# One over the rms of x by a transposed write and a broadcast read, V's tiles at another offset, the last row pair in banks of its own, and a reciprocal with a fixed place

## The chip, the cores and the metric

The kernel runs on one core of a Trainium2 chip. The time is the device time of one execution in microseconds (us), the median of three runs. A core has five engines with instruction streams of their own: TensorE (PE, matrix products; its weight loads are listed as PEld), VectorE (DVE), ScalarE (ACT), GpSimd (POOL) and SyncE (SP), which mainly starts DMA transfers. An engine runs its stream in order; streams wait for each other through semaphores. PE writes its results into eight PSUM banks of 128 partitions by 512 float32, which DVE and ACT read.

## The reference

One layer of a hybrid encoder on x of 512 tokens by 2048 features, batch 1:

```python
h = rms_norm(x, norm_w)                       # 1/sqrt(mean(x*x)) per token, times norm_w
proj = h @ w_in                               # 2048 -> 4608: q | k | v | gate | lru input | lru gate
attn_out = attention_group(q, k, v, ...)      # 8 heads, 2 kv heads, head size 128, qk-norm, axial rope
lru_out = lru_group(xr, ...)                  # conv of 4 taps, two gated scans, forward and backward
mixed = concat(rms_norm(attn_out) * silu(g_attn), rms_norm(lru_out) * silu(g_lru))
out = x + mixed @ w_out                       # 2048 -> 2048
```

All arrays are float32, and the result is wanted in nearly that precision.

## The kernel before, in words

Every matrix operand is split into a high part (rounded to the float32r format, which PE takes in one pass) and a low part (the rest), and every product is three matmuls: high by high, high by low, low by high (`mm3`, lines 153 to 155, and `product`, line 1035). A weight chunk is 256 rows by 512 columns: SP loads it (`wraw`, line 206) into a ring of three slots (`wr`), ACT writes the high part (`wh`, line 218) and DVE the low part (`wl`, line 219). A chunk is 24 matmuls of a projection.

The projections run one after another on PE, whose instruction order is the written one: the lru input in two halves of 512 columns (`a1` and `a2`), k and v, q in two halves, then the lru gates and the attention gates, which are woven with the attention; last the output product, which goes by seven products of half size (Strassen's scheme) with sums of weights built by DMA. x itself comes in eight chunks of 256 features. They are turned to features by tokens, by PE (line 253) or by 32 by 32 block transposes and a round trip through DRAM (lines 281, 289, 296), and split in two (line 339), while `a1` is already being computed from them.

x is not scaled by 1/rms before the projection. The factor is applied to the result when it leaves PSUM: per partition, where tokens lie on partitions (`rstd`, 128 by 4), and by a full tile `rbc` (128 by 512, the same row of 512 token factors on each partition), where tokens lie along the row (`evac_bc`, line 471). `rows` makes `rbc` from `rstd`: DVE splits `rstd` (lines 357, 358), multiplies an identity by each column (line 360, two 128 by 512 tiles), PE sums them over the partitions with a matrix of ones (line 367, two matmuls), and DVE copies the bank to `rbc` (line 368). Its first part is issued at step (4, 3) of `a1` (chunk 4, column block 3), the matmuls at step (7, 0). Seven small loads of vectors (`vec_load`, line 180, into `vec_st`) are issued at step (4, 2), turned by PE at step (7, 1) (line 189).

`a2` takes the four PSUM banks that `a1` leaves, so that its first matmul needs the first `evac_bc` of `a1`.

Attention works by heads. Per head and block of 128 queries: scores (`mm<-kt,q`), maximum, exponent, division, a block transpose, and a round trip through DRAM (`u`, `pd`, `pt`) that gives the weights as keys by queries, split in `ph` and `pl`. `values` multiplies them with V: twelve matmuls per head whose stationary operand is V's high or low tile (`mm<-ph,v`). V's tiles come from `aside`, which takes a tile of 528 floats and uses the 512 that begin 8 floats (32 bytes) in.

`spread` gives the factors of the two group norms: two matmuls with ones (line 831), a square root by ACT (832), and four reciprocals of 128 columns by DVE (835). The second use is in the last gate projection, from `later()`. The order of ACT and DVE is made there by a planner, by priorities; `issue_after` and `behind` put one instruction behind another of the same engine, without a wait.

At the end of the output product, three products Q3, P2 and Q4 of the right-hand columns finish one after another, each with its last two of eight steps and a closing addition by DVE from PSUM (line 1066) and a store (line 1058). Each has two banks, one per 128 rows of the pair. For Q4, the last, the second bank's addition is cut in two column halves, the first stored through ACT's queue and the second through SP's. Here ACT, DVE, SP and POOL also run in the written order.

Of the kernel before, what the change touches and what calls it, by code (L numbers as in the profile page):

```python
# [11 lines left out]
F32 = mybir.dt.float32  # L12
F32R = mybir.dt.float32r
# [4 lines left out]
P = 128  # L18
SEQ = 512
DM = 2048  # L20
KT = DM // P
NT = SEQ // P
HD = 128
NH = 8
NKV = 2
# [11 lines left out]
AHEAD = 600  # L37
# [11 lines left out]
H = 256  # L49
# [14 lines left out]
def hybrid_kernel(  # L64
# [53 lines left out]
    def nm(s):  # L118
        cnt[0] += 1
        return f"{s}_{cnt[0]}"  # L120
# [4 lines left out]
    def k2(dt=F32, shape=(P, SEQ)):  # L125
        return pools["lru"].tile(list(shape), dt, tag="k2", bufs=LRU_K2, name=nm("k2"))
# [13 lines left out]
    def pj():  # L140
        return ps.tile([P, SEQ], F32, tag="pj", name=nm("pj"))

    def mm():
        return ps.tile([P, SEQ], F32, tag="mm", name=nm("mm"))

    def const(shape, name, dt=F32):
        return cp.tile(list(shape), dt, tag=name, name=name)
# [22 lines left out]
    def vec_load():  # L170
        for lo, src in (
            (R_CW, conv_w.rearrange("t o (n p) -> (t o n) p", p=P)),
            (R_CB, conv_b.rearrange("(n p) -> n p", p=P)),
            (R_BA, lru_ba.rearrange("d (n p) -> (d n) p", p=P)),
            (R_BX, lru_bx.rearrange("d (n p) -> (d n) p", p=P)),
            (R_LAM, lru_lambda.rearrange("d (n p) -> (d n) p", p=P)),
            (R_AN, attn_norm_w.rearrange("(n p) -> n p", p=P)),
            (R_LN, lru_norm_w.rearrange("(n p) -> n p", p=P)),
        ):
            nc.sync.dma_start(vec_st[lo : lo + src.shape[0], :], src)  # L180
# [62 lines left out]
    def behind(those):  # L243
        stack = ExitStack()
        for ins in those:
            stack.enter_context(tc.issue_after(ins))
        return stack
# [101 lines left out]
    rstd = const([P, NT], "rstd")  # L349
    rbc = const([P, SEQ], "rbc")  # L350

    def rows(dst, col, dg):

        shape = [P, NT, P]
        part = [const([P, NT], nm("part")) for _ in range(2)]
        parts = [dg() for _ in part]
        nc.vector.tensor_copy(part[0].bitcast(F32R), col)
        nc.vector.tensor_sub(part[1], col, part[0])
        for c, d in zip(part, parts):
            nc.vector.tensor_mul(  # L360
                d, ident[:, None, :].broadcast_to(shape), c[:, :, None].broadcast_to(shape)
            )
        yield
        pb = mm()
        for k, d in enumerate(parts):
            d = d.rearrange("p t q -> p (t q)")
            nc.tensor.matmul(pb, ones_r, d, start=k == 0, stop=k == 1)
        nc.vector.tensor_copy(dst, pb)
        yield

    def xstats():
        s = const([P, NT], "xsum")
        nc.vector.reduce_sum(s, ssq, axis=AX.X)
        rsqrt_mean(rstd, s, DM, NT)
        yield from rows(rbc, rstd, lambda: k2(F32R, (P, NT, P)))

    def proj_feat(c0, acc, first=None, given={}, take=None):

# [273 lines left out]
    def kv(es):  # L654
        turned_k = sent(norm_rope(es, NKV, rk), NKV)
        yield 20
        opened("wx", "right")
        for t in range(NT):
            vv = es[t][:, NKV * HD :]
            vt = aside(  # L660
                lambda *a: pools["qkv"].tile(*a, tag="v", bufs=NT, name=nm("v")), 2 * NKV * HD // H
            )
            vh[t], vl[t] = vt[:, 0, :], vt[:, 1, :]
            nc.scalar.copy(vh[t], vv)
            nc.vector.tensor_sub(vl[t], vv, f(vh[t]))
        yield from lru_squares()
        yield 2
        drain(turned_k)
        yield 6
        pair = landed(asides.pop(0))  # L670
        for h in range(NKV):
            yield (12, 4)[h]
            kt = pools["qkv"].tile([P, 2, SEQ], F32R, tag="kt", bufs=NKV, name=nm("kt"))
            kth[h], ktl[h] = kt[:, 0, :], kt[:, 1, :]
            those = split_head(pair, h, kth[h], ktl[h])
        parts = halved(
            sums["l"],
            lambda: pools["rope"].tile([P, SEQ], F32R, tag="kv", bufs=NT, name=nm("kv")),
            those,
        )  # L680
        yield 4
        spread(gbc, parts, NB * P)
# [141 lines left out]
            nc.vector.tensor_sub(lo, src, f(hi))  # L824
        return hi, lo

    def spread(dst, parts, n):

        pb = mm()
        for k, part in enumerate(parts):  # L830
            nc.tensor.matmul(pb, ones_r, part, start=k == 0, stop=k == 1)  # L831
        nc.scalar.activation(dst, pb, AF.Sqrt, scale=1.0 / n, bias=eps[:, :1])
        for t in range(NT):
            ts_ = slice(t * P, (t + 1) * P)
            nc.vector.reciprocal(dst[:, ts_], dst[:, ts_])  # L835

    gbc = const([P, SEQ], "gbc")

# [12 lines left out]
    def seven(pair, hi, lo):  # L851
# [7 lines left out]
        for to, part in ((slice(0, 3), src[:, 1:4]), (slice(3, 7), res)):  # L859
            nc.scalar.copy(hi[:, to], part)  # L860
            nc.vector.tensor_sub(lo[:, to], part, f(hi[:, to]))

    def aside(tile_of, n):

        t = tile_of([P, n * H + 16], F32R)
        return t[:, 8 : 8 + n * H].rearrange("p (n e) -> p n e", e=H)

    def kept(pool, i):
        return [
# [144 lines left out]
    def outputs(work):  # L1014
# [11 lines left out]
            if u < len(feeds):  # L1026
                next(feeds[u])

        def product(dst, i, k, b, n):
            ah, al = (t[:, k] for t in mixed[i][1])  # L1030
            bh, bl = (t[:, n] for t in b)
            for s in range(2):
                ts_ = slice(s * P, (s + 1) * P)
                for j, (lh, rh) in enumerate(((ah, bh), (ah, bl), (al, bh))):
                    nc.tensor.matmul(  # L1035
                        dst[s], lh[:, ts_], rh, start=i == 0 and j == 0, stop=i == 7 and j == 2
                    )

        def banks(*kinds):
# [9 lines left out]
        for g in range(2):  # L1049
# [6 lines left out]
            def leave(t, j, queue, e0=0, e1=SEQ):  # L1056
                c0 = (2 * g + j) * SEQ
                queue.dma_start(of[tokens[t], c0 + e0 : c0 + e1], xs[j][:, t, e0:e1])

            def last(t0, j, acc, cut=1):  # L1060
                for s in range(2):
                    n = cut if s else 1
                    for e0 in range(0, SEQ, SEQ // n):
                        e1 = e0 + SEQ // n
                        to = xs[j][:, t0 + s, e0:e1]
                        nc.vector.tensor_add(to, to, acc[s][:, e0:e1])  # L1066
                        queue = nc.scalar if e1 < SEQ else nc.sync
                        leave(t0 + s, j, queue if g else nc.gpsimd, e0, e1)

            p1, q5, q6, q7 = banks(*((mm, mm, pj, pj), (pj, mm, mm, pj))[g])  # L1070
            for i in range(NP):
# [52 lines left out]
            for i in range(NP - 2 * g):  # L1124
                u = 16 * g + NP + i
                for (dst, k, b, n), (t0, j) in zip(takes, ends):
                    product(dst, i, k, parts[u][b], n)
                    if i == NP - 1:
                        last(t0, j, dst)
                    if k == P2:  # L1130
                        if i in added:
                            next(rs[added.index(i)])
                        if i in (2, 3):
                            next(rs[i])
                        feed(u + 2)
                feed(u + 2)
                feed(u + 3)

        for (dst, k, b, n), (t0, j) in zip(takes, ends):
            for i in (NP - 2, NP - 1):  # L1140
                product(dst, i, k, parts[24 + i][b], n)
            last(t0, j, dst, 2 if k == Q4 else 1)

# [63 lines left out]
    for step in proj_feat(C_XR, a1, first, given):  # L1209
        if step is None:  # L1210
            with tc.high_priority():
                first.append(wsplit(raw, 1))
                xturn(xc, 1)
            xsquare(xc, 0)
            move(None)
            given[1] = wload(w_in, 2 * P, C_XR)
            continue
        c, e = step
        move(step)
        if (c, e) == (1, 2):  # L1220
            s2.close()
        if (c, e) == (4, 2):
            with tc.high_priority(AHEAD):
                vec_load()
        if (c, e) == (7, 1):
            columns(vec, vec_st)
        if (c, e) in ((4, 3), (KT // 2 - 1, 0)):
            with tc.high_priority(AHEAD), tc.issue_after(split_done[-1][1]):
                next(stats)

    s1.close()
# [119 lines left out]
    def later():  # L1351
        with tc.high_priority():
            parts = halved(sums["a"], lambda: fin_s(dt=F32R))
        yield 2
        with tc.high_priority():
            spread(gbc, parts, NH * HD)
        yield 4
        for pair in ap_[:2]:
            normed(pair)
        yield 4  # L1360
        todo = gate(late, ap_[:2], R_AN, fin_s)
        for _ in range(3):
            yield next(todo)
        build(4, ap_[0], [hring.tile([P, 7, H], F32R, name=nm(t)) for t in ("mh", "ml")])
        yield from todo
        for pair in ap_[2:]:
            normed(pair)
# [78 lines left out]
```

## Time and profile before

| | |
|---|---|
| time, median of 3 runs (range) | 630.35 us (630.19 to 630.4) |
| the profiled execution: its time, its span | 630.3 us, 628.2 us |
| granted TensorE clock, mean | 0.999 |
| PE busy | 622.0 us, 2755 matmuls |
| DVE busy | 494.6 us |
| ACT busy | 353.1 us |
| DMA | 127.61 MB, mean 203 GB/s |

The span is the time from the first to the last instruction in the trace; 2.1 us of the execution lie outside of it. Lines like L219 are lines of the kernel's file, and names such as `wl` are its tiles. A row of the timeline gives start, duration, engine, line, operation, the tile written and those read, its size and the count; the end of a row in brackets is idle time of the engine just before it and what ended that. A row of the chain of waits gives start, duration and what ran. SPq is SP's stream of transfer starts.

### The profile page before, as it was taken

The page shows a single profiled execution, that of the slowest core. Times are in us where ns is not written, and L with a number is a line of the kernel's source. Part 1 is how long each engine was busy: PE and PEld are TensorE (multiplying, and loading weights), DVE is VectorE, ACT ScalarE, POOL GpSimd, SP SyncE. Part 2 cuts the span into 40 slices and gives each one's busy share as a digit, 9 for nine tenths or more (in the row PEclk, how much of TensorE's full clock was granted, in tenths as well). Part 3 has the DMA queues.
Part 4 walks back from the last instruction along what each step waited for, and adds up shares of the span by engine and source line. Part 5 has one row for each costly group of instructions (what it writes and reads, how often), then busy time and mean ns, then how long its engine had stood idle before and what let it go on. Part 6 is the DMA issues. An engine that isn't in the chain of part 4 may idle for free.

```text
span 628.2 us, 8273 instructions
## 1 busy us (share of the span) xinstructions
PE 622.0 (99%) x2755; PEld 512.5 (82%) x2755; DVE 494.6 (79%) x794; ACT 353.1 (56%) x618; POOL 101.4 (16%) x134
## 2 busy tenths in 40 slices
PE   9999999999999999999999999999999999999997
PEld 7888888888888888888888888887888888888885
DVE  5958979986699875987887888549978866886885
ACT  3674899379946823555475447438436643444441
POOL 0000210112002622522122232100120101110010
PEclk9999999999999999999999999999999999999999
DMA  8878785859774599479668646922996777896252
GB/s 284 281 209 263 176 202 172 176 134 192 237 234 135 172 255 227 109 214 267 183 170 254 194 150 185 268 69 67 280 232 204 224 254 244 287 340 213 68 201 100
DMA packets 73594, 127.61 MB, mean 203 GB/s; under 512 B 6616, under 2 KB 29264, under 8 KB 73552
## 3 DMA queue, kind: packets, MB, share of 16 engines
q1 hardware_dynamic: 65664, 109.65, 55.9%
q0 software_dynamic: 7712, 17.31, 14.2%
q8 instruction: 21, 0.34, 0.2%
q14 instruction: 21, 0.17, 0.1%
q10 hardware_dynamic: 176, 0.14, 0.1%
HBM read 110.29 MB, written 37.75 MB: 236 GB/s over the span
## 4 chain that ended last, share of the span: by engine, by line
PE 98%; DVE 1%; issue 0%; DVEq 0%; POOL 0%; POOLq 0%
PE pj L155 20%; PE pj L153 20%; PE pj L154 20%; PE mm L1035 14%; PE pj L1035 10%; PE mm L155 4%; PE mm L153 3%; PE mm L154 3%; PE pj L388 1%; PE mm L253 1%; PE mm L1153 1%; DVE gbc L835 1%; DVE wl L219 0%; DVE cb L1066 0%; PE mm L831 0%
## 5 line engine op out<-in xcount | busy, mean ns | idle before, releaser
L155 PE MATMUL pj<-x,wl 128*128 128x512 f32 x376 | 146.8, 390 | 0.4 <-DVE wl L219 0.3
L153 PE MATMUL pj<-x,wh 128*128 128x512 f32 x376 | 147.0, 391 | 0.0
L154 PE MATMUL pj<-x,wh 128*128 128x512 f32 x376 | 146.6, 390 | 0.0
L218 ACT CAST wh<-wr 128x512 fp32r<-128x512 f32 x143 | 85.4, 617 | 81.9 <-PE pj L154 32.0
L219 DVE TENSOR_TENSOR wl<-wr,wh 128x512 fp32r<-128x512 f32 x144 | 100.0, 724 | 21.2 <-ACT wh L218 19.9
L887 ACT CAST wh<-wr 128x1024 fp32r<-128x1024 f32 (+1 forms) x72 | 60.5, 860 | 77.3 <-PE mm L1035 35.9
L888 DVE TENSOR_TENSOR wl<-wr,wh 128x1024 fp32r<-128x1024 f32 (+1 forms) x72 | 68.5, 985 | 30.7 <-ACT wh L887 30.5
L155 PEld LDWEIGHTS pj<-x,wl 128*128 128x128 f32 x376 | 70.6, 188 | 16.1 <-DVE wl L219 1.3
L153 PEld LDWEIGHTS pj<-x,wh 128*128 128x128 f32 x376 | 70.6, 188 | 14.7
L154 PEld LDWEIGHTS pj<-x,wh 128*128 128x128 f32 x376 | 70.6, 188 | 14.7
L153 PE MATMUL pj<-wh,x 128*128 128x512 f32 x192 | 74.8, 389 | 0.0
L155 PE MATMUL pj<-wh,x 128*128 128x512 f32 x192 | 74.8, 389 | 0.0
L154 PE MATMUL pj<-wl,x 128*128 128x512 f32 x192 | 74.8, 389 | 0.0
L911 POOL DMA_DIRECT2D t<-in_w_out_dram x40 | 33.5, 901 | 161.3 <-DMA t<-in_w_out_dram 99.5
L1035 PE MATMUL mm<-wl,mh 128*128 128x512 f32 x128 | 49.8, 389 | 0.0
L1035 PE MATMUL mm<-wh,mh 128*128 128x512 f32 x128 | 49.8, 389 | 0.0
L1035 PE MATMUL mm<-wh,ml 128*128 128x512 f32 x128 | 49.8, 389 | 0.0
L153 PEld LDWEIGHTS pj<-wh,x 128*128 128x128 f32 x192 | 36.0, 188 | 7.5
L154 PEld LDWEIGHTS pj<-wl,x 128*128 128x128 f32 x192 | 36.0, 188 | 7.5
L155 PEld LDWEIGHTS pj<-wh,x 128*128 128x128 f32 x192 | 36.0, 188 | 7.4
L708 POOL TENSOR_SCALAR p<-p,sm 128x512 f32<-128x512 f32 x32 | 24.3, 764 | 90.0 <-DVE sm L707 90.0
L1035 PE MATMUL pj<-wh,mh 128*128 128x512 f32 x96 | 37.4, 390 | 0.0
(200 smaller groups left out, 1038.2 us busy)
## 6 DMA issues: line engine op xcount, KB each, us to landing
wr<-in_w_in_dram SPq DMA_DIRECT2D x71, 512.0 KB, 5.1
wr<-in_w_out_dram SPq DMA_DIRECT2D x24, 512.0 KB, 5.1
t<-in_w_out_dram POOLq DMA_DIRECT2D x40, 256.0 KB, 6.8
wr<-t SPq DMA_DIRECT2D x40, 256.0 KB, 5.9
pd<-u SPq DMA_DIRECT2D x16, 512.0 KB, 3.0
pt<-pd SPq DMA_DIRECT2D x64, 128.0 KB, 3.9
t<-in_w_out_dram SPq DMA_DIRECT2D x24, 256.0 KB, 5.5
t<-t SPq DMA_DIRECT2D x16, 256.0 KB, 5.7
```

Source lines behind the costliest of these rows:

```text
L153: nc.tensor.matmul(acc, lh, rh, start=start, stop=False)
L154: nc.tensor.matmul(acc, lh, rl, start=False, stop=False)
L155: nc.tensor.matmul(acc, ll, rh, start=False, stop=stop)
L218: copy(hi, raw[:, k, :]).ins,
L219: nc.vector.tensor_sub(lo, raw[:, k, :], f(hi)).ins,
L253: nc.tensor.transpose(pt[:, t * P : (t + 1) * P], xc[:, t, ks], ident)
L388: nc.tensor.matmul(acc[e], w[:, e * P : (e + 1) * P], x_[k], start=k == 0 and j == 0, stop=False,)
L708: last_pool[0] = nc.gpsimd.tensor_scalar(p, p, sm, 0.0, op0=ALU.mult, op1=ALU.add).ins
L887: nc.scalar.copy(hi[:, to], b)
L888: nc.vector.tensor_sub(lo[:, to], b, f(hi[:, to]))
L911: nc.gpsimd.dma_start(dst, src, accum_op=ALU.add)
L1035: nc.tensor.matmul(dst[s], lh[:, ts_], rh, start=i == 0 and j == 0, stop=i == 7 and j == 2)
```

## The change

Four edits, independent of each other.

1. `rows` goes. `xstats` now puts `rstd` into the first four columns of a zeroed 128 by 32 tile, turns it by 32 by 32 blocks (one DVE instruction), so that the factors of the tokens lie along rows, writes the 512 numbers by four DMAs (four partitions of 32 numbers each) to a row in DRAM, and reads that row back to all 128 partitions as `rbc` by one DMA. The four writes, the seven vector loads and the broadcast read stand in this order on SP at step (5, 0); the vector loads stood at (4, 2).
2. V's tiles are taken without `aside`: 512 floats, beginning at the tile's start.
3. The last reciprocals are put behind the second `wl` split of one weight chunk on DVE (`those`).
4. For Q4's second bank, the partial sum of the first six steps is added to the output tile as soon as they are done; the last two steps go by column halves of 256, each into a fresh PSUM bank, and each half is added and stored as soon as it is there.

```diff
-    def rows(dst, col, dg):
-
-        shape = [P, NT, P]
-        part = [const([P, NT], nm("part")) for _ in range(2)]
-        parts = [dg() for _ in part]
-        nc.vector.tensor_copy(part[0].bitcast(F32R), col)
-        nc.vector.tensor_sub(part[1], col, part[0])
-        for c, d in zip(part, parts):
-            nc.vector.tensor_mul(
-                d, ident[:, None, :].broadcast_to(shape), c[:, :, None].broadcast_to(shape)
-            )
-        yield
-        pb = mm()
-        for k, d in enumerate(parts):
-            d = d.rearrange("p t q -> p (t q)")
-            nc.tensor.matmul(pb, ones_r, d, start=k == 0, stop=k == 1)
-        nc.vector.tensor_copy(dst, pb)
-        yield
...
         rsqrt_mean(rstd, s, DM, NT)
-        yield from rows(rbc, rstd, lambda: k2(F32R, (P, NT, P)))
+        across, along = k2(shape=(P, B)), k2(shape=(P, B))
+        nc.gpsimd.memset(across, 0.0)
+        nc.vector.tensor_copy(across[:, :NT], rstd)
+        nc.vector.transpose(along, across)
+        yield
+        row = dram.tile([1, SEQ], F32, name="rows", tag="rows")
+        to = row.rearrange("o (t b r) -> (o b) t r", b=NQ, r=B)
+        for b in range(NQ):
+            nc.sync.dma_start(to[b], along[b * B : b * B + NT])
+        yield
+        nc.sync.dma_start(rbc, row.broadcast_to([P, SEQ]))
+        yield
...
-            vt = aside(
-                lambda *a: pools["qkv"].tile(*a, tag="v", bufs=NT, name=nm("v")), 2 * NKV * HD // H
-            )
+            vt = pools["qkv"].tile([P, 2, NKV * HD], F32R, tag="v", bufs=NT, name=nm("v"))
...
-    def spread(dst, parts, n):
+    def spread(dst, parts, n, those=()):
...
         for t in range(NT):
             ts_ = slice(t * P, (t + 1) * P)
-            nc.vector.reciprocal(dst[:, ts_], dst[:, ts_])
+            with behind(those):
+                nc.vector.reciprocal(dst[:, ts_], dst[:, ts_])
...
-    def aside(tile_of, n):
-
-        t = tile_of([P, n * H + 16], F32R)
-        return t[:, 8 : 8 + n * H].rearrange("p (n e) -> p n e", e=H)
...
-        def product(dst, i, k, b, n):
+        def product(dst, i, k, b, n, ss=range(2), es=slice(None), ends_=(0, NP - 1)):
             ah, al = (t[:, k] for t in mixed[i][1])
             bh, bl = (t[:, n] for t in b)
-            for s in range(2):
+            for s in ss:
                 ts_ = slice(s * P, (s + 1) * P)
                 for j, (lh, rh) in enumerate(((ah, bh), (ah, bl), (al, bh))):
                     nc.tensor.matmul(
-                        dst[s], lh[:, ts_], rh, start=i == 0 and j == 0, stop=i == 7 and j == 2
+                        dst[s][:, es], lh[:, ts_], rh[:, es],
+                        start=i == ends_[0] and j == 0, stop=i == ends_[1] and j == 2,
                     )
...
-            def last(t0, j, acc, cut=1):
-                for s in range(2):
-                    n = cut if s else 1
-                    for e0 in range(0, SEQ, SEQ // n):
-                        e1 = e0 + SEQ // n
-                        to = xs[j][:, t0 + s, e0:e1]
-                        nc.vector.tensor_add(to, to, acc[s][:, e0:e1])
-                        queue = nc.scalar if e1 < SEQ else nc.sync
-                        leave(t0 + s, j, queue if g else nc.gpsimd, e0, e1)
+            def last(t0, j, acc, ss=range(2), e0=0, e1=SEQ):
+                for s in ss:
+                    to = xs[j][:, t0 + s, e0:e1]
+                    nc.vector.tensor_add(to, to, acc[s][:, e0:e1])
+                    queue = nc.scalar if e1 < SEQ else nc.sync
+                    leave(t0 + s, j, queue if g else nc.gpsimd, e0, e1)
...
-                    product(dst, i, k, parts[u][b], n)
+                    if g and i == NP - 3 and k == Q4:
+                        product(dst, i, k, parts[u][b], n, (0,))
+                        product(dst, i, k, parts[u][b], n, (1,), ends_=(0, i))
+                        nc.vector.tensor_add(xs[j][:, t0 + 1], xs[j][:, t0 + 1], dst[1])
+                    else:
+                        product(dst, i, k, parts[u][b], n)
...
-            for i in (NP - 2, NP - 1):
-                product(dst, i, k, parts[24 + i][b], n)
-            last(t0, j, dst, 2 if k == Q4 else 1)
+            pieces = [(dst, (0, 1), 0, SEQ, (0, NP - 1))]
+            if k == Q4:
+                pieces = [(dst, (0,), 0, SEQ, (0, NP - 1))] + [
+                    ((None, pj()), (1,), e0, e0 + H, (NP - 2, NP - 1)) for e0 in (0, H)
+                ]
+            for to, ss, e0, e1, ends_ in pieces:
+                for i in (NP - 2, NP - 1):
+                    product(to, i, k, parts[24 + i][b], n, ss, slice(e0, e1), ends_)
+                last(t0, j, to, ss, e0, e1)
...
-        if (c, e) == (4, 2):
-            with tc.high_priority(AHEAD):
-                vec_load()
...
-        if (c, e) in ((4, 3), (KT // 2 - 1, 0)):
+        if (c, e) == (4, 3):
             with tc.high_priority(AHEAD), tc.issue_after(split_done[-1][1]):
+                next(stats)
+        if (c, e) == (5, 0):
+            with tc.high_priority(AHEAD):
+                next(stats)
+                vec_load()
                 next(stats)
...
-            spread(gbc, parts, NH * HD)
+            spread(gbc, parts, NH * HD, split_done[turn_of[0] - 2][1:])
```

In this diff `P` is 128, `NT` 4, `B` 32, `NQ` 4, `H` 256, `NP` 8, `SEQ` 512.

## The prediction

> **What bounds the kernel now.** I read first the busy times and the chain of waits on the page, then PE's own waits, then the timeline at the four places that the diff touches.
>
> ```profile
> PE 622.0 (99%) x2755; PEld 512.5 (82%) x2755; DVE 494.6 (79%) x794; ACT 353.1 (56%) x618; POOL 101.4 (16%) x134
> ...
> PE 98%; DVE 1%; issue 0%; DVEq 0%; POOL 0%; POOLq 0%
> ```
>
> ```profile
> PE pj L155 <- DVE wl L219: 0.3, 1, 0.3
> ```
>
> PE is the chain: of 628.2 us it is busy 622.0, and once its work has begun the only wait that its list shows is one late weight split, 0.3. So this change can gain in four ways only: fewer matmuls, matmuls that follow each other faster, that late split, and the tail behind the last matmul. Removed work on DVE or SP gains nothing by itself, and added work costs only where it makes PE wait. The sum is made against the profiled execution, 630.3 us with a span of 628.2, thus 2.1 outside of it; the median, 630.35, is the same within 0.05.
>
> The unit is PE's step. Rows of the chain:
>
> ```profile
> 429.28 0.46 PE mm L831 x2
> ...
> 543.29 2.72 PE mm L1035 x12
> ```
>
> 2.72/12 = 0.2267 us per matmul of 512 columns. A matmul's own row says 0.39, since they overlap; starts have to be compared, not durations.
>
> **Edit 1, rbc without PE.** Rows of PE around the two matmuls that go:
>
> ```profile
> 50.14 0.62 PE L367 MATMUL mm<-k,ones_r 128*128 128x512 f32 x2
> 50.60 0.40 PE L153 MATMUL pj<-x,wh 128*128 128x512 f32 x1
> ...
> 51.98 0.25 PE L189 MATMUL mm<-ident,vec_st 104*128 104x104 f32 x1
> ...
> 54.87 0.39 PE L153 MATMUL pj<-x,wh 128*128 128x512 f32 x1
> ```
>
> They take 50.60 - 50.14 = 0.46, and the six matmuls behind them 1.38 where six steps are 1.36: 0.48 us gained. What must hold is that rbc comes in time. The matmul at 54.87, 18 steps behind 50.60, is the first of a2; it takes the bank that the first L471 empties. In the changed kernel that is at 54.4. Rows of DVE, of SP's queue, and a wait of SP:
>
> ```profile
> 37.64 0.17 DVE L357 CAST part<-rstd 128x4 fp32r<-128x4 f32 x1 [1.45 <-POOL rstd L347]
> ...
> 51.41 1.28 DVE L219 TENSOR_TENSOR wl<-wr,wh 128x512 fp32r<-128x512 f32 x2
> ...
> 53.38 1.88 DVE L471 TENSOR_TENSOR ev<-pj,rbc 128x512 f32<-128x512 f32 x3
> ```
>
> ```profile
> 36.63 0.40 SPq L206 DMA_DIRECT2D wr<-in_w_in_dram  x1
> 37.12 1.83 SPq L296 DMA_DIRECT2D xu<-xd  x4
> 39.00 0.43 SPq L180 DMA_DIRECT2D vec_st<-in_conv_w_dram  x1
> ...
> 41.91 0.31 SPq L180 DMA_DIRECT2D vec_st<-in_lru_bx_dram  x1
> ...
> 43.69 0.28 SPq L180 DMA_DIRECT2D vec_st<-in_lru_norm_w_dram  x1
> 44.07 0.40 SPq L206 DMA_DIRECT2D wr<-in_w_in_dram  x1
> ...
> 48.66 4.43 SPq L206 DMA_DIRECT2D wr<-in_w_in_dram  x3
> ```
>
> ```profile
> SPq L180 <- DMA wr<-in_w_in_dram: 1.7, 1, 1.7
> ```
>
> An L471 takes 1.88/3, about 0.63, so rbc must be there by 53.7. rstd is there at 37.6. A memset on POOL, a copy and a block turn of at most 128x32 on DVE are of the kind of the 0.17; with their hand-overs I put them before 39.0, when SP comes free. DVE idled up to 37.64 and loses L357 to L360 there and L368 later, so these cost nothing; without that gap they would stand before a weight split, some 0.5 us. The fourth small load waits 1.7 us until 41.91, for the weight load issued at 36.63, eight transfers earlier: about eight are out at a time. So three writes leave where three vector loads leave now, from 39.00 on; the fourth write and four vector loads take the five places from 41.91 to 44.07; the other three and the read follow at 0.38 (43.69 to 44.07). The read leaves at 45.6, and behind it a2's first weight load at 46.0 for 44.07, then the lru weights and the next chunk, also some two us late.
>
> ```profile
> vec_st<-in_lru_bx_dram SPq DMA_DIRECT2D x1, 8.0 KB, 2.6
> k<-in_lru_wa_dram SPq DMA_DIRECT2D x4, 128.0 KB, 3.7
> ```
>
> ```profile
> DMA to landing us min/median/max: 3.5/5.4/6.9
> ```
>
> The first two rows are small transfers near this place; the third is for the weight loads (512 KB) between 20 and 70 us. A write I price as the vector load, 2.6: the fourth lands at 44.5, ahead of the read. The read (256 KB) lies between the lru weights' 3.7 and the longest weight load, 6.9: rbc at 49.3 to 52.5, before 53.7. The first chunk lands at 51.4, at most 52.9; its first high and low part take some 0.65 each (half of 1.28), so 54.2 at the latest, for a low part wanted at 54.4 plus two steps, 54.9. The next chunk is wanted 24 steps on, at 59.9; issued by 51.5 it lands by 58.4. The vector loads leave by 45.3, land by some 48 to 49 and are wanted at 51.5. So the delays are covered, by 0.7 us at the worst landings seen. The edit is worth 0.48; if the cover fails, it costs the difference (rivals).
>
> The Trainium skill, "DMA: Bandwidth & Descriptors" (Specifications; Anatomy of one DMA), speaks against these writes: pieces below 512 bytes go by read-modify-write, and most of a transfer's fixed 2 us is the wait for the receipt, longest in HBM. No run shown has a row of a 128-byte write; this bears on the late-DMA rival's chance.
>
> **Edit 2, V's offset.** Rows of PE in the second head's product with V, and two groups of its matmuls:
>
> ```profile
> 317.21 0.40 PE L155 MATMUL mm<-kt,q 128*128 128x512 f32 x1
> 317.45 0.39 PE L153 MATMUL mm<-ph,v 128*128 128x512 f32 x1
> ...
> 322.09 0.39 PE L155 MATMUL pj<-x,wl 128*128 128x512 f32 x1
> ```
>
> ```profile
> L153 PE MATMUL mm<-ph,v 128*128 128x512 f32 x32 | 12.7, 397 | 0.0
> ...
> L153 PE MATMUL mm<-kt,q 128*128 128x512 f32 x32 | 12.5, 389 | 0.0
> ```
>
> The 21 steps from 317.21 to 322.09 take 4.88, where 21 times 0.2267 are 4.76: 0.12 us are lost in a head, in twelve steps with V and some behind them, and nothing is waited for. Scores (`kt,q`), the same kind of group, run at 389 ns where V's run at 397. V alone begins 32 bytes into its tile, and that is what the edit removes. Eight heads: 0.96 us at most, 0 if the offset isn't the cause. I take 0.80, near the top: the offset sets V apart, but after L367 too a group left 0.02 behind it, and eight of these (0.16) may stay.
>
> **Edit 3, the reciprocals.** Rows of all engines:
>
> ```profile
> 432.24 1.13 ACT L218 CAST wh<-wr 128x512 fp32r<-128x512 f32 x2
> ...
> 434.71 3.39 DVE L835 RECIPROCAL gbc<-gbc 128x128 f32<-128x128 f32 x4
> ...
> 437.98 0.39 PE L154 MATMUL pj<-x,wh 128*128 128x512 f32 x1
> 438.01 2.43 DVE L219 TENSOR_TENSOR wl<-wr,wh 128x512 fp32r<-128x512 f32 x4
> 438.70 0.50 PE L155 MATMUL pj<-x,wl 128*128 128x512 f32 x1 [0.33 <-DVE wl L219]
> ...
> 439.98 0.39 PE L154 MATMUL pj<-x,wh 128*128 128x512 f32 x1
> ```
>
> The high parts are ready at 433.4, but DVE does four reciprocals first, and PE waits for the low part. From 437.98 to 439.98 are six steps, 1.36 us, in 2.00: 0.64 lost. When `later` calls `spread`, the projection has begun its first chunk with three fetched ahead, so the last but one chunk split is its third. It is also the one that stalls: L831 at 429.28 stands two column blocks (12 steps) into the first chunk, 36 steps before the third, which begins at 429.28 + 0.46 + 8.16 = 437.9. The pin puts both its low parts, 1.3 us, ahead of the reciprocals: they end at 436.0, the reciprocals at 439.4, the next pair of low parts at 440.7, wanted one chunk on, at 443.4. gbc comes 1.3 us later.
>
> ```profile
> 445.97 1.23 DVE L840 TENSOR_TENSOR av<-av,gbc 128x1024 f32<-128x1024 f32 x1
> ```
>
> Its first reader runs at 445.97. So 0.64 gained; the bounds are 0.64 and 0, if another split is late next.
>
> **Edit 4, the tail.** Rows of PE, of DVE, of PE's turns at the start, and the group of weight loads:
>
> ```profile
> 622.04 0.39 PE L1035 MATMUL mm<-wh,mh 128*128 128x512 f32 x1
> ...
> 623.17 0.39 PE L1035 MATMUL mm<-wh,ml 128*128 128x512 f32 x1
> ```
>
> ```profile
> 622.92 1.43 DVE L1066 TENSOR_TENSOR cb<-cb,mm 128x512 f32<-128x512 f32 x3 [1.35 <-PE mm L1035]
> ```
>
> ```profile
> 15.78 1.03 PE L253 MATMUL mm<-ident,b 128*128 128x128 f32 x8
> ```
>
> ```profile
> L1035 PEld LDWEIGHTS mm<-wh,mh 128*128 128x128 f32 x128 | 24.0, 188 | 5.0
> ```
>
> Now the last matmul starts at 623.17 and ends at 623.56, and the two half additions behind it end with DVE's row at 622.92 + 1.43 = 624.35; these 0.79 are a hand-over and two times about 0.38. In the changed kernel the second bank's six matmuls become twelve of 256 columns from 622.04 on, each with its weight load, and one half addition is left behind the last. No row shows a 256-column matmul of this type; half of 0.2267 is 0.113. From below, turns with a load each take 1.03 for eight, less the last one's pipeline of some 0.2 to 0.3, so about 0.11 apart: loads as close as that are possible. From above, 0.188, a load's own row, if loads did not overlap. I take 0.12, nearest to the half. Then the last starts at 622.04 + 11 x 0.12 = 623.36, ends 0.28 later (0.39 less half a step), and its addition at 623.64 + 0.45 = 624.09: 0.26 gained; at 0.11 0.37, at 0.188 0.49 lost, even at 0.143. Stores and landing stay. The added full addition (about 0.68, L1066's size) comes when Q4's sixth step ends, 36 steps before the last matmul, near 615.3; DVE's split behind it, of Q4's eighth step, is wanted 27 steps later, six us: covered.
>
> By the Trainium skill, "TensorE: Matmul & The Clock Gate" (Back-to-back issue gap), 256 columns take 262 cycles at 2.4 GHz, 0.109 us, and the sum would be 0.12 more; its 518 cycles for 512 are 0.216, where the trace has 0.2267, and no run here shows the 256.
>
> **Sum.** 0.48 + 0.80 + 0.64 + 0.26 = 2.18 us. Span 626.0, time 628.1. A change of 0.2% (1.26 us) is about what a measurement of this kernel tells from none.
>
> **The rivals.** *V's loss isn't the offset* but belongs to a group that starts behind other operands: 0.80 stays, 628.9. For it: the loss runs on after V's last step. Against: scores show none, and after L367 it is 0.02. Chance 0.14.
>
> *Another split falls behind long work*: the planner orders DVE anew around the edits. The trace prices one such place at 0.64; two or three take 1.3 to 1.9: 629.4 to 630.0. For it: DVE is 79% busy. Against: one late split now in the whole list. Chance 0.13.
>
> *The DMA route is late*, which ends slower: SP stands at the read until the fourth write has landed, and the weight load stands behind it. PE waits once that load leaves after 54.9 - 1.3 - 5.4 = 48.2, thus when the writes land after 47.8, 3.3 us later than I have it. To lose the 2.18 and 1.26 more they must land after 51.2; at 51.5 PE stalls 3.7 at the start of a2, and the time is 631.8. Against: the longest landing there is 6.9, for 512 KB. Chance 0.11.
>
> *The half pieces bind on loads* (0.188): 0.49 lost for 0.26 gained, 628.9. Chance 0.06. The forecast keeps 0.56.
>
> **Numbers.** The forecast alone: 627.6 to 628.8 (V at 0.96 or 0.3, the tail at 0.37 or even). Range 627.2 to 630.1: it takes in V without gain, the bound pieces and the missed splits, and below also the stalls too small for the list; it leaves out the late DMA and part of the edges. Faster by over 0.2% (below 629.1): forecast, V, pieces and little else, 0.77. Within: the splits, 0.13. Slower: 0.10, nearly all the late DMA.
>
> **What would show it.** PE with 2755 - 2 + 6 = 2759 matmuls and no L367; V's group at 389 ns like the scores'; no wait of PE on `wl` near 437; starts of the 256-column matmuls 0.12 apart and one half addition behind the last. For edit 1: L471 waits for PE, not for a DMA, and PE nowhere near 54. The prediction is wrong if PE waits at the start of a2, if V's rows keep their spacing, or if waits on `wl` stand where none were.

## The result, and the profile after

The changed kernel takes 633.84 us (median of 6 runs, 633.51 to 634.07) against 630.28 (629.92 to 630.4) for the kernel before on the same chip: a ratio of 1.0057 [1.0044, 1.0070], slower by 3.56 us. The prediction was 628.1, faster. The profiled execution took 634.07, its span is 631.9.

Lines have moved: the product's matmuls are L1019 (L1035 before), its closing additions L1048 (L1066), its stores L1043, the reciprocals L824 (L835), `evac_bc` L461 (L471). The new writes are L364, the broadcast read L366, the copy and the turn L358 and L359.

The busy times of the page, its chain of waits by engine, and the whole list of PE's waits, in the changed kernel:

```profile
PE 626.5 (99%) x2759; PEld 512.1 (81%) x2759; DVE 493.0 (78%) x792; ACT 353.2 (56%) x618; POOL 101.3 (16%) x135
...
PE 99%; ACT 0%; DVE 0%; POOL 0%; issue 0%; POOLq 0%
```

```profile
PE mm L1146 <- POOL ones L161: 1.2, 1, 1.2
```

PE has the 2759 matmuls that were forecast, the late split near 437 has left the list, and what is left is a wait of 1.2 at the very start. No other engine became the bound. Yet PE is busy for 4.5 us more than before (622.0). So PE's list has no wait that could hold the loss; the matmuls themselves follow each other more slowly. The chain around the start of the output product shows it (start, duration, what ran):

```profile
472.32 0.23 PE pj L154
472.54 0.23 PE pj L155
472.77 2.76 PE mm L1019 x12
475.53 2.80 PE pj L1019 x12
478.33 2.80 PE mm L1019 x12
```

Twelve matmuls take up to 2.80, thus 0.2333 each; before, twelve of the same took 2.72 (0.2267) throughout. The groups of one form agree (busy time, mean ns of one), in the kernel before:

```profile
L1035 PE MATMUL mm<-wh,mh 128*128 128x512 f32 x128 | 49.8, 389 | 0.0
```

and in the changed kernel:

```profile
L1019 PE MATMUL mm<-wh,mh 128*128 128x512 f32 x126 | 49.5, 393 | 0.0
...
L153 PE MATMUL mm<-ph,v 128*128 128x512 f32 x32 | 12.6, 394 | 0.0
```

393 ns stands against 389 in the product, and V's group, which was to come down from 397 to 389, is at 394. PE runs the same matmuls in the same order in both, but for those that the edits change, so the starts of one and the same matmul can be compared. This gives the places: from 42 to 65 us the changed kernel gains 0.53, from 65 to 429 it loses 2.45, around 438 it gains 0.65, and from 453 to 611 it loses 2.51.

The edits did what they were to do. SP's and DVE's rows of the changed kernel around `rbc`:

```profile
37.63 0.17 DVE L358 COPY k<-rstd 128x4 f32<-128x4 f32 x1 [1.46 <-POOL rstd L347]
37.83 0.21 DVE L359 STREAM_TRANSPOSE k<-k 128x32 f32<-128x32 f32 x1
...
39.52 2.47 SPq L364 DMA_DIRECT2D rows<-k  x4
...
45.69 0.35 SPq L366 DMA_DIRECT2D rbc<-rows  x1
46.14 0.58 SPq L206 DMA_DIRECT2D wr<-in_w_in_dram  x1
...
52.12 1.91 DVE L461 TENSOR_TENSOR ev<-pj,rbc 128x512 f32<-128x512 f32 x3
```

The read leaves at 45.69 and the weight load at 46.14 (forecast 45.6 and 46.0), and L461 waits for no DMA.

### The profile page after: what moved, and what is told of

The parts are those of the page before. It is cut to its first block, busy times and chain, and to the rows that moved or that the text cites. A ratio compares the mean times of both kernels' runs of the same rounds, so it can differ in the third digit from the quotient of the medians.

```text
span 631.9 us, 8288 instructions
## 1 busy us (share of the span) xinstructions
PE 626.5 (99%) x2759; PEld 512.1 (81%) x2759; DVE 493.0 (78%) x792; ACT 353.2 (56%) x618; POOL 101.3 (16%) x135
## 4 chain that ended last, share of the span: by engine, by line
PE 99%; ACT 0%; DVE 0%; POOL 0%; issue 0%; POOLq 0%
PE pj L153 21%; PE pj L155 21%; PE pj L154 21%; PE mm L1019 14%; PE pj L1019 11%; PE mm L155 4%; PE mm L153 3%; PE mm L154 3%; PE pj L378 1%; PE mm L253 1%; PE mm L1146 0%; PE mm L819 0%; ACT x L258 0%; DVE cb L1048 0%; PE mm L189 0%
## 5 line engine op out<-in xcount | busy, mean ns | idle before, releaser
L1019 PE MATMUL mm<-wh,mh 128*128 128x512 f32 x126 | 49.5, 393 | 0.0
L1019 PE MATMUL mm<-wh,ml 128*128 128x512 f32 x126 | 49.4, 392 | 0.0
L1019 PE MATMUL mm<-wl,mh 128*128 128x512 f32 x126 | 49.3, 391 | 0.0
L1019 PE MATMUL pj<-wh,mh 128*128 128x512 f32 (+1 forms) x100 | 38.9, 389 | 0.0
```

Source lines behind the costliest of these rows:

```text
L1019: nc.tensor.matmul(dst[s][:, es], lh[:, ts_], rh[:, es], start=i == ends_[0] and j == 0, stop=i == ends_[1] and j == 2,)
```

## The experiments

What the prediction leaves out is where tiles lie. `rows` owned two constant tiles, `part`, of 16 bytes per partition; each takes 32. With them gone, everything laid out behind them on that side of the memory (the weight chunks and x's parts among it) starts 64 bytes lower. The tiles laid out from the other side (q, the keys, V, a part of the weight chunks and of the mixed activations) stay. By the program's addresses, all operands of the 512-column matmuls before start 192 bytes past a multiple of 256; only V's four tiles (32, 96, 160 and 224 past it) and the matrix of ones stand elsewhere. In the changed kernel some start at 128 and some at 192. The theory, "operand places", is that PE's step depends on where its two operands start, relative to each other. The rival was that the new order of DVE and SP, or the new traffic, costs the 6 us.

**Put 64 bytes back (e1_gap64).** The changed kernel and one unused tile:

```diff
-        rsqrt_mean(rstd, s, DM, NT)
+        rsqrt_mean(rstd, s, DM, NT); const([P, 16], "gap")
```

> The changed kernel with an unused 64-byte tile among the constants, where the two tiles of rows lay: every pool on the left side of SBUF lies where it lay before, 64 bytes higher than in the changed kernel; no instruction is added or moved. Theory A (offset): PE's step is 0.227 us when the moving and the stationary operand start at the same offset within 128 bytes and about 0.233 when they are 64 apart; the whole loss comes from the shift. Then the time is the predicted 628.1 (627.6 to 628.8), below both kernels, and PE's step is 0.227 in the output product. Theory B (work): the added DMAs, waits and the new order cost it; the time stays at 633.8.

Measured: 627.73 (627.37 to 627.87), ratio 0.9960 [0.9945, 0.9975] to the kernel before, 6.1 us below the changed kernel (the kernel before took 630.28 beside the one and 630.19 beside the other); the order of instructions is the same. The busy times and the chain there:

```profile
PE 620.4 (99%) x2759; PEld 513.2 (82%) x2759; DVE 492.3 (79%) x792; ACT 352.8 (56%) x618; POOL 101.0 (16%) x135
```

```profile
471.93 2.72 PE pj L1019 x12
474.65 2.72 PE mm L1019 x12
```

```profile
L153 PE MATMUL mm<-ph,v 128*128 128x512 f32 x32 | 12.5, 389 | 0.0
```

All three answers are the forecast's: 0.2267 a step, V at 389, and a time within 0.4 of the 628.1. An unused tile is the whole difference between slower and faster than before; this version and the next, whose ranges overlap, are the fastest of this study.

**Or move the other side (e2_right64).** Instead of the gap, the first tile of the other side grows by 64 bytes:

```diff
-    opened("pad", "right").tile([P, 8], F32, name="pad")
+    opened("pad", "right").tile([P, 24], F32, name="pad")
```

> The changed kernel with the first tile on the right side of SBUF 96 bytes instead of 32: the pools on the right move down by 64 bytes, those on the left stay where the change put them. Theory A, if the two operands' offsets count relative to each other: 628.1 as with the gap, since all tiles then start at 0 modulo 128. If the absolute place counts (0 modulo 128 is bad, 64 good): slower than 633.8, up to 636, since more operands then lie at 0. Theory B: 633.8.

Measured: 627.92 (627.38 to 628.04), ratio 0.9962 [0.9948, 0.9976]. So it is the place of one side relative to the other, not an absolute one.

**The kernel before, shifted (e3_before64, e4_before128, e5_before256).** None of the four edits, only an unused tile of 64, 128 or 256 bytes. The edit for 64 (the other two have 32 and 64 for the 16, which counts floats):

```diff
-    last_pool = [None]
+    last_pool = [None]; const([P, 16], "gap")
```

> The kernel before with an unused 64-byte tile among its constants and nothing else: the left pools move up by 64 bytes against the right ones. Theory A: slower by what the changed kernel lost against the prediction, 633.84 - 628.1 = 5.7, so about 636 (634.5 to 637), with PE's step at about 0.230 to 0.233 where operands come from both sides. Theory B: 630.3, as before.

> The kernel before with an unused tile of 128 bytes. Theory A, with 128 bytes as the period: 630.3, no change, and PE's step 0.2267. If the period is longer, or any move of the pools costs: about 634 to 636.

> The kernel before with an unused tile of 256 bytes among its constants. The 128 bytes cost as much as the 64, so 128 is not the period. Theory A with a period of 256 bytes in the distance of the moving from the stationary operand: 630.2, as before, and PE's step 0.2267. Rival: any move of the left pools against the right ones costs: 634.4, as with 64 and 128.

Measured: 634.41, ratio 1.0067 [1.0052, 1.0082], for 64 bytes; 634.53, 1.0069 [1.0054, 1.0084], for 128; 630.18, 1.0002 [0.9992, 1.0011], for 256. Rows of the chain with 64, 128 and 256 bytes:

```profile
476.51 2.76 PE pj L1035 x12
```

```profile
478.31 2.80 PE mm L1035 x12
```

```profile
476.84 2.72 PE mm L1035 x12
```

So the kernel before loses 4.2 us by 64 idle bytes and no work. The expectation with 128 as the period was wrong: 128 bytes cost as much as 64, and 256 cost nothing. For 64 the expectation was 1.6 us too high, and its range was missed by 0.1.

**V alone (e6_v_alone, e7_v_by64).** The kernel before with edit 2 alone (e6), and with V 64 instead of 32 bytes into its tile (e7). The edit of e7:

```diff
-        t = tile_of([P, n * H + 16], F32R)
-        return t[:, 8 : 8 + n * H].rearrange("p (n e) -> p n e", e=H)
+        t = tile_of([P, n * H + 32], F32R)
+        return t[:, 16 : 16 + n * H].rearrange("p (n e) -> p n e", e=H)
```

> The kernel before with edit 2 alone: V's tiles begin at the tile's start, where moving and stationary operand are then a multiple of 256 bytes apart. Theory A: the loss of 0.12 us in each head goes, 629.2 (629.0 to 629.5), and V's matmuls stand 0.227 apart. Rival, the loss belongs to a group that starts behind other operands: 630.2.

> The kernel before with V 64 bytes into its tile instead of 32, so that V is again at a multiple of 64 bytes but 64 or 192 from the weights of the keys within 256. Theory A (distance within 256): V's matmuls stay slow, 0.230 to 0.235 apart, time 630.2 as before. Rival B (a multiple of 64 bytes is enough, as the change's words put it): the gain of edit 2, 629.2.

Measured: 629.33, ratio 0.9989 [0.9979, 0.9998], for edit 2 alone; 629.93, 0.9996 [0.9987, 1.0006], for 64 bytes. V's group (shortest, median, longest ns) in the first and in the second:

```profile
L153 PE MATMUL mm<-ph,v x32: 387/389/397, 301.3 to 418.5; 128*128 128x512 f32 x32
```

```profile
L153 PE MATMUL mm<-ph,v x32: 393/396/399, 300.7 to 418.3; 128*128 128x512 f32 x32
```

A start at a multiple of 64 is not enough. Between 270 and 453 us the matched matmuls of edit 2 alone gain 0.74.

**Places one by one (m1_offsets).** This kernel leaves out the whole layer: 18 blocks of 64 matmuls of 128 by 512 on PE, in one execution, each matmul with another stationary tile than the one ahead of it. Per block, the stationary operands start s bytes and the moving ones m bytes behind the same place. One block in short, with s and m in floats (the file has their numbers):

```python
for n in range(64):
    w = st[:, s + n % 2 * P : s + n % 2 * P + P]
    nc.tensor.matmul(acc, w, mv[:, m : m + 512], start=n == 0, stop=n == 63)
```

> PE alone: 18 blocks of 64 matmuls of 128x512 with a new stationary operand each, all on the same data, with the two operands' starts moved by bytes; it leaves out the whole layer and stores the last two sums. Theory A: 64 steps take 14.5 us where moving minus stationary is a multiple of 256 bytes (0, 256, 512, 1024, and 64 with 64), and 14.7 to 15.0 at 32, 64, 96, 128, 160, 192 and 224; the same difference gives the same time wherever the stationary operand lies. Rival (absolute place): blocks with the stationary operand at 64 or 128 differ from those at 0 at the same difference. Open: distances of 16 and 240.

Measured, in the chain (start, duration, block). (s, m) in bytes: L61 is (0, 64), L65 (0, 128), L73 (0, 256), L75 (64, 64), L77 (64, 0), L81 (192, 0), L85 (0, 240), L87 (0, 512), L91 (0, 0) at the end:

```profile
38.06 14.66 PE even L61 x64
...
67.64 14.93 PE even L65 x64
...
127.44 14.53 PE even L73 x64
141.97 14.55 PE odd L75 x64
156.52 14.93 PE even L77 x64
...
186.32 14.65 PE even L81 x64
...
215.80 15.14 PE even L85 x64
230.94 14.53 PE odd L87 x64
...
259.98 14.52 PE odd L91 x64
```

14.52/64 is the step of the kernel before, 0.2269 with its edges. It stands at every distance m - s that is a multiple of 256, and for (64, 64) as for (0, 0). The first block, at (0, 0) too, took 17.65, since its first matmuls were slower, and is left out here. A distance of 64 costs 2 ns a matmul, a little less than expected, and it is the same 14.65 for (0, 64) and (192, 0); 128 and -64 cost 6 to 7, 240 costs 10. The blocks at 32, 96, 192 and 224 took 14.93 or 14.94, at 160 14.99 and at 16 14.82. No wait and no other engine is needed for it.

**Edit 1 alone, without and with the gap (e8_rows_alone, e9_rows_alone_gap64).** Whether the price hangs on edit 1 alone:

> The kernel before with edit 1 alone (x's 1/rms by turn, writes and read); V, the reciprocals and the tail as before. It removes the two small constant tiles, so the left-side pools start 64 bytes lower, as in the changed kernel. Theory 'operand distance': the edit's own 0.84 us (measured between 42 and 65 us in e1) is gained, and the 4.2 to 6.1 us that a shift of 64 bytes cost (e3; the changed kernel against e1) are lost: 633.6 to 635.5, with PE's step at 228 to 232 ns outside V's groups. Rival 'the shift costs only together with the other edits' (V's new place, the split tail): 629.3 to 629.9 and the step at 226.7.

> As e8, with 64 unused bytes kept where the two constant tiles lay. Theory 'operand distance': the pools stand as before, only the edit's own 0.84 is left: 629.3 to 629.9, step 226.7 outside V's groups. If the edit's DMAs or its turn cost something that the place of the tiles hides, it is not below 630.2.

Measured: 634.83, ratio 1.0072 [1.0055, 1.0089], without; 629.74, 0.9993 [0.9983, 1.0002], with 64 idle bytes. (The second also computes `rstd` twice, on POOL, by a line left standing: two instructions more, at 37.19 and 37.48, which can only delay the edit's copy.) Chains of the first and of the second:

```profile
476.05 2.80 PE pj L1025 x12
```

```profile
473.28 2.72 PE pj L1026 x12
```

Edit 1 alone brings the loss, 4.5 us, and not by its copy, turn, writes or read: with the gap, the same work is no slower than the kernel before, and the matched matmuls around 50 us gain its 0.48. The 64 bytes are worth 5.1 here, against 6.1 with all four edits; most of the difference lies between 270 and 429 us, where edit 2 gains (0.88 here, 1.58 there). The rival falls.

**Neighbours at different places (m2_places).** One part was left. Grouped by the operands' addresses, 458 matmuls of the changed kernel had distances of 64 or 192 and followed each other by 232 to 233 ns. But the 2210 with equal places (within 256 bytes, as everywhere here; the few steps over 260 ns are left out) took 228.4 in the mean, not 226.8 as in e1, and most of the loss, about 3.6 of 6.1, is theirs. They were slow near matmuls at another place; PE's rows in the changed kernel, where three score matmuls (both operands at 192) stand between projection matmuls (both at 128):

```profile
267.65 0.39 PE L155 MATMUL pj<-x,wl 128*128 128x512 f32 x1
267.87 0.39 PE L153 MATMUL mm<-kt,q 128*128 128x512 f32 x1
...
268.57 0.39 PE L153 MATMUL pj<-x,wh 128*128 128x512 f32 x1
...
269.26 0.39 PE L153 MATMUL pj<-x,wh 128*128 128x512 f32 x1
```

From 267.87 to 269.26 are six steps in 1.39, where six are 1.36. So blocks of 96 were run, again in one execution, in which neighbours differ. This kernel leaves out the whole layer too. One block in short (the file has the pattern written out):

```python
for n in range(96):
    s, m = pattern[n % len(pattern)]
    nc.tensor.matmul(acc, st[:, s + n % 2 * P : s + n % 2 * P + P], mv[:, m : m + 512],
                     start=n == 0, stop=n == 95)
```

> Leaves out the whole layer: 13 blocks of 96 matmuls of 128 by 512 on PE alone, each with a new stationary tile; (s, m) are the bytes by which stationary and moving operand lie past the same place. All at (0,0) is 96 x 0.2267 = 21.76 us. Question: in the changed kernel matmuls whose two operands have equal places ran at 228.4 ns in the mean, not 226.7, above all near those at another place (the six from 267.87 to 269.26 took 1.39, not 1.36). Theory 'a change of place between neighbours costs too': 3 of 12 at (64,64) and 9 at (0,0) takes 8 x 0.03 to 0.05 more, 22.0 to 22.2; 3 of 6 takes 22.2 to 22.6; by 256 nothing, 21.76. Rival 'only the pair of one matmul counts, the rest in the layer is something else': every block with equal pairs takes 21.76. With 3 of 6 at (0,64), as in the layer's q and k projections (232.7 on both kinds): theory 22.3, rival 48 x 2.2 ns more, 21.87; with 3 of 6 at (64,0): theory 22.3 or more, rival 48 x 6.6 ns more, 22.08.

Measured, in the chain. L59: all at (0, 0). L61: 3 of 12 at (64, 64), the rest at (0, 0). L63: 3 of 6. L65: 12 of 24. L69: 3 of 12 at (256, 256). L73: 3 of 6 at (0, 64). L75: 3 of 6 at (64, 0):

```profile
30.36 21.76 PE odd L59 x96
52.12 22.13 PE even L61 x96
74.25 22.29 PE odd L63 x96
96.54 21.95 PE even L65 x96
...
140.73 21.78 PE even L69 x96
...
184.58 22.35 PE even L73 x96
206.94 22.29 PE odd L75 x96
```

Pairs at equal places, but neighbours 64 bytes apart, cost 0.37 for eight visits, 0.046 a visit (a visit is a run of matmuls at another place and the way back). With 3 of 6 the visits stand closer and cost 0.033 each; 3 of 6 at (128, 128), a block not shown, took 22.07, 0.019 each. The starts around one visit, with 3 of 12, follow each other by 228, 229, 232, 240, 227, 230, 236, 229, 232, 231 ns, and only then by 227 again. In the layer the second visit, at 271.3, has 229, 229, 232, 240, 226, 231, 236, 228, 233, 231. So PE alone makes the pattern that the layer has, and "only the pair of one matmul counts" falls. By 256 bytes it costs nothing.

The changed kernel's trace says how much of its loss this is. Of the 2210 matmuls at equal places, 1061 have the same place as the ten ahead of them and the one behind: these take 226.8 ns in the mean, as in e1. The other 1149, with a neighbour elsewhere, hold all of the 3.6 us.

## Why the prediction was wrong

**The failed step** is "The unit is PE's step", 2.72/12 = 0.2267 us, carried over to the changed kernel for all matmuls that the diff does not touch. The step is a property of where operands lie, and edit 1, by removing two constant tiles, moved one side of the memory by 64 bytes. With it falls "added work costs only where it makes PE wait": PE lost time without waiting. In place of the 2.18 us gained, 3.56 were lost; e1, which differs by that place alone, gives the price as 6.1 (633.84 - 627.73); where V was out of place already, it is 4.2 (e3, the other way) and 5.1 (e8 against e9). The view that could have told it was quoted: V's group at 397 beside the scores' at 389, with V "32 bytes into its tile", said that an offset of an operand changes the step. I used it for the edit that repairs such an offset and did not ask which edit makes one. The rows said more: the last score ahead of V's group is at its own right place, and yet its step is 235 ns (317.21 to 317.45), 228 with V in place (e6). So "scores show none" does not hold for the score next to V, and a neighbour's part could be seen.

The rivals did not hold it either. The slower one, a late DMA route, fell: L461 waits for no DMA in the changed kernel. "Another split falls behind long work" and "half pieces bind on loads" did not happen.

The terms of the sum, measured with the places right (matched matmuls of e1 and the kernel before):

- Edit 1, 0.48 predicted: 0.48 in every run that has the edit (the changed kernel, e1, e2, e8, e9). Its cover held.
- Edit 2, 0.80 predicted, 0.96 at most: 0.95 in e1, 0.74 alone. The size was right and the cause only half: not the 32 bytes into the tile, but the distance of V from the other operands and their neighbours, within 256 bytes. At 64 bytes in, V's group stayed at 396.
- Edit 3, 0.64 predicted: 0.65. DVE's order in e1 is as drawn, the two low parts, the reciprocals, then the next pair:

```profile
433.40 1.28 DVE L219 TENSOR_TENSOR wl<-wr,wh 128x512 fp32r<-128x512 f32 x2
434.61 3.38 DVE L824 RECIPROCAL gbc<-gbc 128x128 f32<-128x128 f32 x4
437.90 1.22 DVE L219 TENSOR_TENSOR wl<-wr,wh 128x512 fp32r<-128x512 f32 x2
```

- Edit 4, 0.26 predicted with 0.12 a piece: 0.26 up to the end of the last addition, and 0.25 more behind it. "Stores and landing stay" did not hold: from that end to the end of the span are 3.57 or 3.58 us in the three kernels with this edit (the changed kernel, e1, e2), 3.81 to 3.83 in the kernel before and e3 to e7 (3.98 in e8 and e9, also without this edit, on a chip of their own). Why is not shown, and no run has edit 4 alone. The 0.45 for the last addition was right (0.46 measured), though "a hand-over and two times about 0.38" gives 0.41. The eleven steps between the first and the last half matmul of e1 take 1.31, 0.119 each:

```profile
620.03 0.28 PE L1019 MATMUL pj<-wh,mh 128*128 128x256 f32 x1
...
621.34 0.28 PE L1019 MATMUL pj<-wh,ml 128*128 128x256 f32 x1
...
621.66 0.42 DVE L1048 TENSOR_TENSOR cb<-cb,pj 128x256 f32<-128x256 f32 x1 [0.29 <-PE pj L1019]
```

For e1 the terms come to 0.48 + 0.95 + 0.65 + 0.51 = 2.59, where 2.46 were measured (630.19 - 627.73). That e1 meets the forecast of 628.1 within 0.4 is in part luck: the tail's 0.25 and V's 0.15 were not in the sum, and in e1 some of it went elsewhere.

The Trainium skill, "TensorE: Matmul & The Clock Gate" (Back-to-back issue gap), gives 0.109 for 256 columns and 0.216 for 512; the trace has 0.119 and, at the best places, 0.2267, so the measured ones stand. What the Trainium skill, "DMA: Bandwidth & Descriptors" (Specifications), says of pieces below 512 bytes did not decide anything: the fourth write was issued at 41.7 and the read left at 45.69, without a wait in SP's rows.

One reading was incomplete without harm. PE's own list had one late split; the list for the weight loads, which the prediction does not show, has two in the kernel before:

```profile
PEld pj L155 <- DVE wl L219: 1.3, 2, 0.8
```

The other one, near 43.7, is gone in e1 to e8, and there in the changed kernel and e9. It does not go with an edit, since e5 has none and keeps the step; what decides it is not shown. In e1 and e6 PE's work also stands 0.5 to 0.8 later by 20 us, which eats its 0.4.

## What to carry to other kernels

Before costing an edit by the step of its matmuls, ask whether it moves tiles: removing or adding a small tile shifts everything allocated behind it. Keep the float32r operands of neighbouring matmuls at the same start within 256 bytes, and when a matmul group is a few ns slower than its like without any wait, look at its addresses first. To compare two kernels edit by edit, give the one with fewer tiles idle bytes, so that the rest stays where it was.

## What was unexpected in the hardware

PE's step of 226.7 ns for 512 columns holds only where the stationary and the moving operand, and the neighbouring matmuls, start at the same place within 256 bytes. A steady distance costs 2 to 10 ns (229 at 64, 233 at 32, 96, 128, 192 and 224, 237 at 240). A visit to a place 64 bytes away and back costs 0.046 us, over some ten steps, and less where visits stand closer. How the two combine is open. With 3 of 6 at (0, 64), 48 times 2.2 ns alone would give 21.87, with sixteen visits (0.53, as at (64, 64)) 22.40, and 22.35 was measured; with 3 of 6 at (64, 0) the same sum, with 48 times 6.4 ns, gives 22.60, and 22.29 was measured. Why 256, which part of the chip is shared there, and whether other types or shapes show it, these runs do not tell.
